# Nineteen pairs of projections by Strassen's seven products, ahead of an attention that takes more of the convolution's taps

## The chip, the cores and the metric

The kernel runs on one core of a Trainium2 chip. The core has a matrix engine (TensorE, PE in the profile; PEld is its weight load), three engines for elementwise work (VectorE is DVE, ScalarE is ACT, GpSimd is POOL), a queue engine that issues transfers (SyncE, SP), an on-chip memory of 128 partitions (SBUF) and an accumulator memory that TensorE writes (PSUM). The metric is the device time of one execution in microseconds; lower is better.

## The reference

One layer of a streaming encoder in float32 for 1024 prompt frames and 32 frames of running streams (TT = 1056 columns in all), model width 1024. What matters here:

```python
h = rmsnorm(x, norm_g)
cols = lambda a, w: h @ w_in[:, a:a + w]
q = rmsnorm(cols(OFF_Q, ATTN_WIDTH).reshape(B, T, N_HEADS, HEAD_DIM), q_g) * (HEAD_DIM ** -0.5)
k = rmsnorm(cols(OFF_K, ATTN_WIDTH).reshape(B, T, N_HEADS, HEAD_DIM), k_g)
v = cols(OFF_V, ATTN_WIDTH).reshape(B, T, N_HEADS, HEAD_DIM)
ga = cols(OFF_GA, ATTN_WIDTH)
u = cols(OFF_UA, CONV_WIDTH) * jax.nn.sigmoid(cols(OFF_UB, CONV_WIDTH))
...
ya = (o_attn.reshape(B, T, ATTN_WIDTH) * jax.nn.silu(ga)) @ w_pa
yb = (jax.nn.silu(layernorm(conv, ln_g, ln_b)) * jax.nn.silu(gb)) @ w_pb
m = jax.nn.sigmoid(ma) * ya + jax.nn.sigmoid(mb) * yb
return x + m @ w_out
```

`o_attn` is causal softmax attention of 16 heads of 64 with a bias from cumulated forget gates, `conv` a causal depthwise convolution of 31 taps over u.

## The kernel before

The activations lie transposed: channels on the partitions, the 1056 frames as columns. x is split once into a rounded part xh and the rest xl, eight groups of 128 channels each. Each of the nine input projections (q, k, v, ga, ub, ua, gb, ma, mb) has 1024 outputs, eight groups f of 128. One projection (g, f) is `steps`: three chunks of 352 columns, for each chunk eight groups kt of input channels, for each kt the three products wh·xh, wl·xh and wh·xl (`mms`, L102), 72 matmuls that accumulate in one PSUM bank a chunk. Its weights, 128 x 1024, arrive by one transfer of 512 KB (`load_raw`); ScalarE rounds them to wh (L91), POOL makes wl = raw - wh in three pieces of 384, 384 and 256 columns (L94).

The stages follow each other: x is prepared while u0 and u1 (ub and ua of group 0 and 1) run; then the value projection (L582, moving operand 260 columns) with u2 inside; k and q with u3 to u6 between; u7; eight groups of ga; the attention of 128 blocks (16 heads by 8 blocks of 128 frames) and four sample groups; then pa, pb and out, three projections of the same kind.

`beat()` stands behind every three matmuls. It counts a tick, runs what `later(n, fn)` set down for that tick, and pays out taps: each beat adds `pace["rate"]` to a credit, and while that is not negative the next tap or chore is issued. A tap is one of the 31 steps y = u[i:] * w + y of a convolution group, one VectorE instruction over 1086 columns (L258; the first of a group on ScalarE, L255), 30 a group, 240 in all. `sums(f)` adds a finished group to the layer norm's mean on VectorE (L235) and its squares on POOL (L241).

A q or k chunk is squared (ScalarE), split (L690 on VectorE), summed over heads by two matmuls with a matrix of ones (L697, L698), made into a reciprocal root (ScalarE), multiplied on (L704, VectorE, from PSUM) and split again, the low part on POOL (L715).

The order on TensorE, VectorE and ScalarE is the program's own up to the attention; from there it is fixed for TensorE alone, and a scheduler sets the rest. In the attention a block's scores (L905, L906) start three blocks ahead into one of two buffers psS; VectorE adds the mask (L908) and takes the maximum (L910), ScalarE the exponential (L913), VectorE the reciprocal (L915), POOL scales P (L916); TensorE turns P (L926) and multiplies it with V (L940). Between blocks `fill(4)` runs four beats of a filler: 22 further projections (gb, ma, six of mb) in all. The last two groups of mb follow the attention.

Of the kernel before, what the change touches and what calls it, by code (L numbers as in the profile page):

```python
# [30 lines left out]
NFILL = 22  # L31
R_U, R_V, R_QK, R_G, R_A = 0.25, 0.17, 0.19, 0.27, 0.12
# [16 lines left out]
def build(tc, xT, xt, wv, wf, ckT, cv, clT, stT, vec, cst, yT, kT, vO, lfO, cpT, csT):  # L49
# [19 lines left out]
    s_m = dram.tile([128, TT], F32, name="s_m")  # L69

    cp = pool("cp")
    wp = pool("wp", 2)
# [3 lines left out]
    rawp = [wp]  # L76
# [11 lines left out]
    def split_w(raw, offset=2000):  # L88
        with tc.high_priority(offset=offset):
            wh = wp.tile([128, KT, 128], F32R, name="wh", tag="wh")  # L90
            nc.scalar.copy(wh, raw)  # L91
            wl = wp.tile([128, KT, 128], F32R, name="wl", tag="wl")
            for k0, k1 in WSP:
                nc.gpsimd.tensor_sub(wl[:, k0:k1, :], raw[:, k0:k1, :], f32(wh[:, k0:k1, :]))  # L94
        return wh, wl
# [40 lines left out]
    def fetch():  # L136

        if plan:
            key = plan.pop(0)
            if not plan:  # L140
                rawp[:] = [wp]
# [28 lines left out]
    sg = pool("sg")  # L170

    def t352(name, bufs):
        return sg.tile([128, CH], F32, name=name, tag=name, bufs=bufs)

    pq = pool("pq", 1, space=PS)
    pps = ExitStack()
    pjA = pool("pjA", 4, stack=pps, space=PS)
# [15 lines left out]
    cvp = pool("cvp", 2, stack=pcv)  # L193
    us = {}
    taps = []
    cvt = [cvp]
# [9 lines left out]
    def shift_of(y):  # L206

        shift = cvp.tile([128, TT], F32, name="shift", bufs=1)
        ones = cvp.tile([128, 128], F32, name="ones", bufs=1)
# [8 lines left out]
        nc.sync.dma_start(s_m, shift)  # L218
# [28 lines left out]

    def conv_taps(f):
        u = us.pop(f)

        def tap(i):
            w = vec_t[:, V_WDW + f * KC + i:V_WDW + f * KC + i + 1]
            if i == 0:
                y = sides["y", f] = cvt[0].tile([128, CW], F32, name="y", tag="y")
# [4 lines left out]
            if f == 7:  # L259
                tc.keep_in_program_order(t)  # L260
            if i == KC - 1:
                kept(f, y)

        items = [lambda i=i: tap(i) for i in range(KC)]
        if f == 7:
            taps.extend(pend + items)
# [11 lines left out]
    def u_tile(f):  # L278
        if f > 2:
            pump(len(taps) - 66)  # L280
        u = us[f] = cvt[0].tile([128, UW], F32, name="u", tag="u", bufs=3 if f < 7 else 1)
# [4 lines left out]
    def u_done(f):  # L286
        u = us[f]
# [71 lines left out]
    os_t = cp.tile([128, 8, TS], F32, name="os_t")  # L359
# [116 lines left out]
    plan.extend([("ub", 1), ("ua", 1), ("v", 0), ("v", 1), ("ub", 2), ("ua", 2), ("v", 2), ("v", 3), ("ub", 3), ("ua", 3)])  # L476
    for f in range(8):
        if f in (2, 4, 6):
            plan.extend([("ub", 3 + f // 2), ("ua", 3 + f // 2)])
        plan.extend([("k", f), ("q", f)])  # L480
    plan.extend([("ub", 7), ("ua", 7)] + [("ga", f) for f in range(8)] + [("gb", 0)])
# [23 lines left out]
    prw = ExitStack()  # L505
    rxs = [pool(f"rx{i}", 1, stack=prw) for i in range(2)]
    rawp.extend(rxs)
# [3 lines left out]
    p2 = ExitStack()  # L511
    u7p = pool("u7p", 1, stack=p2, side="right")
    pv = ExitStack()
    zp = pool("zp", 1, stack=pv, side="right")
    z = zp.tile([128, 9, H], F32, name="z")
# [45 lines left out]
    for c in range(4):  # L561
        if c == 2:
            pace["rate"] = R_U
            u_proj(2, pj)
            while ("y", 0) not in sides or len(taps) > 62:
# [28 lines left out]
    fp = pool("fp", 1, stack=pv, side="right")  # L594
# [3 lines left out]
    def small(name):  # L598
        return fp.tile([128, NZ], F32, name=name, tag=name)

    lf = fp.tile([128, 9, H], F32, name="lf")
    lfs = lf, lf.rearrange("p a b -> p (a b)")

    def log_sigmoid():
        lf, lff = lfs
        az, ee, s2, ac = small("az"), small("ee"), small("s2"), small("ac")
# [19 lines left out]
        chores.extend([(0.3, op) for op in ops] + [(0.0, forget_sums)])  # L626
# [620 lines left out]
```

## Time and profile before

| | us |
|---|---|
| median of 3 runs | 1405.24 (1404.52 to 1405.70) |
| profiled execution, its own time | 1405.11 |
| span of the profiled execution | 1403.3 |
| x, u0, u1 | 0 to 72 |
| value projection with u2 | 72 to 193 |
| q, k, u3 to u6 | 193 to 503 |
| u7, ga | 503 to 613 |
| attention with 22 fillers | 613 to 1106 |
| two gates, pa, pb, out | 1106 to 1403 |

The span is the time from the first to the last instruction; the profiled execution's own time lies 1.8 us above it. A row of a group reads: line, engine, operation, tile written <- tiles read, shape, count | busy us, mean ns of one | idle time of the engine ahead of them and who ended it. A row of windows gives a stretch, its length, and for each engine its busy time and count. Matmuls overlap, so the duration of one is longer than the distance from one to the next.

### The profile page before, as it was taken

Reading aid. Unit: us, or ns where it says so; the run is one execution under the profiler, and the core shown is the slowest. Engines: PE = TensorE matmul, PEld = TensorE weight load, DVE = VectorE, ACT = ScalarE, POOL = GpSimd, SP = SyncE. Lnnn points to the kernel's source line nnn. Section 1 sums busy time; section 2 is a strip of 40 time slices with the busy share of each in tenths; the row PEclk is TensorE's granted clock in tenths of the full one; section 3 lists DMA queues with packets and bytes.
Section 4 is the critical chain, followed back from the end, with each engine's and each line's share of the span. In section 5 each row is a group of like instructions: output and inputs, shape, how many; then the busy total and the mean of one; then the engine's idle time right before and its main releaser. Section 6 shows DMA issues by size and latency. Waiting matters only on the chain.

```text
span 1403.3 us, 23422 instructions
## 1 busy us (share of the span) xinstructions
PE 1390.1 (99%) x8999; PEld 1303.6 (93%) x8999; DVE 866.0 (62%) x1199; ACT 604.2 (43%) x1180; POOL 617.5 (44%) x541
## 2 busy tenths in 40 slices
PE   8999999999999999999999999999999999999999
PEld 7999999999999999998888888878888999999998
DVE  6687787888898998646655656644444497132111
ACT  6322334646464642245454546544554455232100
POOL 2324254557585875343433433232332366254320
PEclk9999999999999999999999999999999999999999
DMA  4242333424342484335545546353532778444431
GB/s 181 92 141 92 119 108 99 160 76 142 106 152 92 138 194 150 111 100 129 148 107 160 146 136 177 101 154 109 155 115 73 276 254 271 143 138 142 150 108 47
DMA packets 102288, 192.77 MB, mean 137 GB/s; under 512 B 17248, under 2 KB 70368, under 8 KB 102176
## 3 DMA queue, kind: packets, MB, share of 16 engines
q1 hardware_dynamic: 102032, 191.21, 44.4%
q8 instruction: 71, 1.16, 0.4%
q14 instruction: 41, 0.34, 0.1%
q10 hardware_dynamic: 144, 0.07, 0.0%
HBM read 125.58 MB, written 65.64 MB: 136 GB/s over the span
## 4 chain that ended last, share of the span: by engine, by line
PE 92%; issue 3%; DVE 2%; ACT 2%; POOL 1%; DMA 1%; SPq 0%; ACTq 0%; POOLq 0%; DVEq 0%
PE pj L102 67%; PE pjv L582 7%; PE po L940 5%; PE ptr L926 4%; PE psS L905 3%; PE psS L906 2%; POOL wl L94 1%; PE pst L698 1%; PE pst L697 1%; PE po L885 0%; DVE y L1082 0%; PE ptx L427 0%; DMA xtok<-xt 0%; ACT xh L429 0%; PE pjs L541 0%
## 5 line engine op out<-in xcount | busy, mean ns | idle before, releaser
L102 PE MATMUL pj<-xh,wh 128*128 128x352 f32 (+2 forms) x1536 | 510.0, 332 | 1.7 <-ACT t L753 1.1
L102 PE MATMUL pj<-xh,wl 128*128 128x352 f32 (+2 forms) x1536 | 494.0, 322 | 1.9 <-POOL wl L94 1.9
L102 PE MATMUL pj<-xl,wh 128*128 128x352 f32 (+2 forms) x1536 | 495.5, 323 | 0.2
L94 POOL TENSOR_TENSOR wl<-raw,wh 128x384 fp32r<-128x384 f32 (+1 forms) x258 | 323.1, 1280 | 258.1 <-ACT wh L91 226.9
L258 DVE SCALAR_TENSOR_TENSOR y<-u,vec_t,y 128x1086 f32<-128x1086 f32 x240 | 382.5, 1594 | 23.7 <-ACT y L255 19.6
L102 PEld LDWEIGHTS pj<-xh,wh 128*128 128x128 f32 x1536 | 289.0, 188 | 10.2 <-ACT t L753 6.6
L102 PEld LDWEIGHTS pj<-xh,wl 128*128 128x128 f32 x1536 | 289.9, 189 | 2.5 <-POOL wl L94 2.2
L102 PEld LDWEIGHTS pj<-xl,wh 128*128 128x128 f32 x1536 | 289.1, 188 | 1.4 <-DVE xl L430 1.2
L916 POOL TENSOR_SCALAR P<-P,nm 128x128 f32<-128x128 f32 (+7 forms) x128 | 107.6, 842 | 283.3 <-DVE nm L915 216.9
L91 ACT CAST wh<-raw 128x1024 fp32r<-128x1024 f32 x86 | 90.1, 1048 | 111.2 <-PE pj L102 80.5
L913 ACT ACTIVATE P<-psS,nm 128x128 f32<-128x128 f32 (+7 forms) x128 | 95.4, 745 | 70.7 <-DVE nm L910 61.5
L910 DVE TENSOR_REDUCE nm<-psS 128x1 f32<-128x128 f32 (+7 forms) x128 | 96.8, 756 | 8.6
L908 DVE TENSOR_TENSOR psS<-psS,cmask 128x128 f32<-128x128 f32 x128 | 38.1, 297 | 100.3 <-PE psS L906 99.3
L929 ACT COPY pt<-ptr 128x512 f32<-128x512 f32 (+3 forms) x128 | 65.0, 508 | 75.8 <-PE ptr L926 75.1
L715 POOL TENSOR_TENSOR ql<-qn,qh 128x352 fp32r<-128x352 f32 (+1 forms) x48 | 66.0, 1374 | 68.0 <-ACT qh L714 54.9
L926 PE MATMUL ptr<-ident,P 128*128 128x128 f32 x576 | 84.2, 273 | 0.0
L940 PE MATMUL po<-pt,V 128*64 128x512 f32 (+1 forms) x384 | 75.8, 530 | 0.0
L926 PEld LDWEIGHTS ptr<-ident,P 128*128 128x128 f32 x576 | 69.1, 140 | 5.6 <-issue 0.4
L582 PE MATMUL pjv<-vwh,xh 128*128 128x260 f32 x256 | 72.5, 283 | 0.0
L582 PE MATMUL pjv<-vwl,xh 128*128 128x260 f32 x256 | 72.4, 283 | 0.0
L582 PE MATMUL pjv<-vwh,xl 128*128 128x260 f32 x256 | 72.3, 282 | 0.0
L905 PE MATMUL psS<-KB,QB 128*128 128x256 f32 (+2 forms) x192 | 70.1, 366 | 0.6 <-ACT t L751 0.6
(200 smaller groups left out, 2237.4 us busy)
## 6 DMA issues: line engine op xcount, KB each, us to landing
raw<-wf SPq DMA_DIRECT2D x88, 512.0 KB
QB<-s_q SPq DMA_DIRECT2D x32, 256.0 KB
KB<-s_k SPq DMA_DIRECT2D x32, 256.0 KB
kT<-qn SPq DMA_DIRECT2D x8, 528.0 KB
s_ga<-t SPq DMA_DIRECT2D x24, 176.0 KB
s_gb<-t SPq DMA_DIRECT2D x24, 176.0 KB
s_ma<-t SPq DMA_DIRECT2D x24, 176.0 KB
s_mb<-t SPq DMA_DIRECT2D x24, 176.0 KB
```

The source lines that it names most:

```text
L91: nc.scalar.copy(wh, raw)
L94: nc.gpsimd.tensor_sub(wl[:, k0:k1, :], raw[:, k0:k1, :], f32(wh[:, k0:k1, :]))
L102: nc.tensor.matmul(ps, a[:, kt, :], b(kt, sl), start=(first and n == 0), stop=(last and n == N - 1))
L258: t = nc.vector.scalar_tensor_tensor(y, u[:, i:i + CW], w, y, op0=ALU.mult, op1=ALU.add)
L582: nc.tensor.matmul(ps[:, :VC], a, b, start=(n == 0), stop=(n == 23))
L715: nc.gpsimd.tensor_sub(ql[:, :n], qn[:, o], f32(qh[:, :n]))
L905: nc.tensor.matmul(ps[:, b, :wm], QB[:, qsl], KB[:, ksl], start=True, stop=False)
L910: nc.vector.tensor_reduce(nm[:, 0:1], ps[:, :nb, :w], axis=AX.XY, op=ALU.max, negate=True)
L913: nc.scalar.activation(P[:, :nk].rearrange("p (b w) -> p b w", b=nb), ps[:, :nb, :w], AF.Exp, bias=nm[:, 0:1], accum_out=nm[:, 1:2])
L916: nc.gpsimd.tensor_scalar(P[:, :nk], P[:, :nk], nm[:, 2:3], 1.0, op0=ALU.mult, op1=ALU.mult)
L926: nc.tensor.transpose(pt[:, 128 * j:128 * j + 128], P[:, 128 * (4 * u + j):128 * (4 * u + j) + 128], ident)
L940: nc.tensor.matmul(po[64 * o:64 * o + 64, q0:], V[:, j + o, hd], p[:, j + o, q0:], start=(j == 0), stop=(j == njb - 2), skip_group_check=True)
```

## The change

Nineteen pairs of projections (ub and ua of groups 4 to 7; k and q of all eight; ga in four pairs; gb 0 to 5 in three), 38 of the 72 input projections, are computed in one stage ahead of the attention by seven products in place of eight (`products`). The weights of the two outputs of a pair and the two halves of the input channels make a 2 x 2 matrix of blocks a11, a12, a21, a22 (128 outputs by 512 channels); the two halves of channels and of columns (HT = 528) of x make b11 to b22. Each product is 2 column halves of HB = 264 by 4 kt by the same 3 terms, 24 matmuls, 168 a pair (L1013), 56 beats. Four PSUM tiles A to D of two banks hold the products; ScalarE takes out p1 and c11, VectorE n2, v3, c22, c21 and c12 (L988 to L1000, 528 columns each).

- *The operands t1 to t4* of x are built during u2 and u3, which now stand behind the whole value projection (`t_build`: joins xh + xl on POOL, sums and splits on VectorE and ScalarE). t1 is written over a quarter of xh and xl, which is kept in DRAM (s_x) and read back at the end of the stage (`restore`).
- *The weights.* Two raw tiles of a pair arrive as before. s2 and s1 start as a plain transfer of 256 KB each; three of the four sums s1, s2, s3 and s4 are then completed by DMAs that add while they write (`w_more`, L758, issued from POOL, 256 KB each, four a pair): s2 += a21, s3 += a11 (in the place of a21), s1 += a22, s2 += a22. The fourth, s4 = s2 + a12, is added by VectorE (`w_sum`, L763). `w_split` rounds each of the seven operands (512 columns) on ScalarE (L769) and takes the rest on POOL (L771), 22 beats ahead of its product.
- *k and q* are normed by halves of 528 columns from SBUF rather than by chunks of 352 from PSUM.
- *Taps.* 63 of the 240 are issued ahead of the pairs, 96 in them (rate 0.1 a beat), 81 in the attention (rate 0.3); before, 28 were issued in the attention. The u of groups 4 to 7 goes to DRAM and is read back when its taps come (`u_load`).
- *The attention* has 16 fillers in place of 22 (gb 6 and 7, ma, six of mb), `fill(3)` in place of `fill(4)`, and a fill ends with a chunk. Two gates follow it as before.

On POOL's order, at one k and q pair and what stands round it. Before (wl is the low half of a weight, ql that of q or k):

```order
L715 TENSOR_TENSOR ql<-qn,qh 128x352
L94 TENSOR_TENSOR wl<-raw,wh 128x384 x2
L94 TENSOR_TENSOR wl<-raw,wh 128x256
L715 TENSOR_TENSOR ql<-qn,qh 128x352
L721 TENSOR_SCALAR qs_t<-qn 128x32
L715 TENSOR_TENSOR ql<-qn,qh 128x320
```

Now (swl is the low half of a block, s_3613 and s_3635 are the tiles of s2 and s1, rawb that of s3, sa the low half of q or k):

```order
L758 DMA s_3613<-wf 128x512
L771 TENSOR_TENSOR swl<-rawb,swh 128x512 x2
L758 DMA s_3613<-wf 128x512
L771 TENSOR_TENSOR swl<-rawa,swh 128x512
L758 DMA rawb<-wf 128x512
L960 TENSOR_TENSOR sa<-qn,sb 128x528
L771 TENSOR_TENSOR swl<-s_3613,swh 128x512
L771 TENSOR_TENSOR swl<-rawb,swh 128x512
L960 TENSOR_TENSOR sa<-qn,sb 128x528
L771 TENSOR_TENSOR swl<-s_3635,swh 128x512
```

DMAs that wait for one another now stand between the subtractions.

On VectorE's order, among the k and q projections before (L258 is a tap):

```order
L704 SCALAR_TENSOR_TENSOR qn<-pj,vec_t,ri 128x352
L690 TENSOR_TENSOR sql<-sqf,sqh 128x352
L258 SCALAR_TENSOR_TENSOR y<-u,vec_t,y 128x1086
L704 SCALAR_TENSOR_TENSOR qn<-pj,vec_t,ri 128x352
L258 SCALAR_TENSOR_TENSOR y<-u,vec_t,y 128x1086
L690 TENSOR_TENSOR sql<-sqf,sqh 128x352
```

and in a pair of k and q now (L261 is a tap; psB to psD are the products' tiles):

```order
L988 TENSOR_TENSOR n<-psB,v 128x528
L261 SCALAR_TENSOR_TENSOR y<-u,vec_t,y 128x1086
L991 TENSOR_TENSOR v<-psC,n 128x528
L956 SCALAR_TENSOR_TENSOR qn<-qn,vec_t,sf 128x528
L994 TENSOR_TENSOR qn<-v,psD 128x528
L261 SCALAR_TENSOR_TENSOR y<-u,vec_t,y 128x1086
L937 TENSOR_TENSOR sa<-sf,sb 128x528
L261 SCALAR_TENSOR_TENSOR y<-u,vec_t,y 128x1086
L997 TENSOR_TENSOR qn<-psC,n 128x528
```

The evacuations, which free the tiles for the next products, stand among the taps, and the norm's two steps now read SBUF alone.

On VectorE's order in the attention, now (L1214 is the mask, L1216 the maximum, L1221 the reciprocal, L1235 a copy of turned P):

```order
L261 SCALAR_TENSOR_TENSOR y<-u,vec_t,y 128x1086
L1221 RECIPROCAL nm<-nm 128x1
L1214 TENSOR_TENSOR psS<-psS,cmask 128x128
L261 SCALAR_TENSOR_TENSOR y<-u,vec_t,y 128x1086
L1216 TENSOR_REDUCE nm<-psS 128x1
L1235 COPY pt_7728<-ptr_9106 128x128
L1214 TENSOR_TENSOR psS<-psS,cmask 128x128
L261 SCALAR_TENSOR_TENSOR y<-u,vec_t,y 128x1086
L1235 COPY pt_7728<-ptr_9135 128x2x128
L1216 TENSOR_REDUCE nm<-psS 128x1
```

A tap stands between a block's mask and its maximum, where before most blocks had none.

The diff, cut to its core:

```diff
@@ -28,8 +28,11 @@
...
-NFILL = 22
-R_U, R_V, R_QK, R_G, R_A = 0.25, 0.17, 0.19, 0.27, 0.12
+NFILL = 16
+R_U, R_V, R_T, R_S, R_A = 0.3, 0.25, 0.19, 0.1, 0.3
+HB = 264
+HT = 2 * HB
+SPILL = 4
...
@@ -623,137 +620,402 @@
...
+    def t_build(j):
+        b11, b12, b22 = [tm.tile([128, HT], F32, name=a, tag=a) for a in ("b11", "b12", "b22")]
+        t1 = t1f[:, j, :]
...
+        def lows():
+            joined(b11, 4 + j, LO)
+            nc.vector.tensor_sub(t3[1][:, j, :], b12, f32(t3[0][:, j, :]))
+
+        return [lambda: nc.vector.tensor_add(b11, f32(xh[:, j, LO]), f32(xl[:, j, LO])),
+                lambda: nc.vector.tensor_sub(t1, b11, b12),
+                lambda: (nc.vector.tensor_sub(b12, b12, b22), nc.scalar.copy(t3[0][:, j, :], b12)),
+                lambda: (nc.vector.tensor_add(b22, b22, t1), nc.scalar.copy(t2[0][:, j, :], b22)),
+                lows,
+                lambda: nc.vector.tensor_sub(t2[1][:, j, :], b22, f32(t2[0][:, j, :])),
+                lambda: (nc.vector.tensor_sub(b11, b11, b22), parts(t4, j, b11))]
...
+    others = [("ub", 4, "ua", 4), ("ub", 5, "ua", 5), ("ub", 6, "ua", 6), ("ub", 7, "ua", 7), ("ga", 0, "ga", 1),
+              ("ga", 2, "ga", 3), ("ga", 4, "ga", 5), ("ga", 6, "ga", 7)]
+    pairs = [("gb", 0, "gb", 1)]
+    for i in range(8):
+        pairs += [("k", i, "q", i), others[i]]
+    pairs += [("gb", 2, "gb", 3), ("gb", 4, "gb", 5)]
...
+    BP = 56
+    LEAD = 22
...
+    def raws_of(i):
...
+        g, f, g2, f2 = pairs[i]
+        with tc.high_priority(offset=2500):
+            w = W[i] = {}
+            for a, key in (("a", (g, f)), ("b", (g2, f2))):
+                w[a] = pw.tile([128, KT, 128], F32, name="raw" + a, tag="raw" + a, bufs=2)
+                nc.sync.dma_start(w[a], wf[WIDX[key]])
+            w["a11"], w["a12"] = w["a"][:, 0:4, :], w["a"][:, 4:8, :]
...
+    def w_first(i, dst, x):
+        w = W[i]
...
+        nc.sync.dma_start(w[dst], half(i, x))
...
+    def w_more(i, dst, x):
+        nc.gpsimd.dma_start(W[i][dst], half(i, x), accum_op=ALU.add)
...
+    def w_sum(i, dst, x, y, home):
+        w = W[i]
+        w[dst] = w[home]
+        nc.vector.tensor_add(w[dst], w[x], w[y])
...
+    def w_split(i, k):
+        raw = W[i][PROD[k][0]]
+        with tc.high_priority(offset=2000):
+            wh = pw.tile([128, 4, 128], F32R, name="swh", tag="swh", bufs=4)
+            nc.scalar.copy(wh, raw)
+            wl = pw.tile([128, 4, 128], F32R, name="swl", tag="swl", bufs=4)
+            nc.gpsimd.tensor_sub(wl, raw, f32(wh))
...
+    def prepare(i):
+        if i >= NP:
+            return
+        s = S0[0] + i * BP
+        for t, dst, x in ((50, "s2", "a11"), (46, "s1", "a21")):
+            at(s - t, lambda dst=dst, x=x: w_first(i, dst, x))
+        for t, dst, x in ((37, "s2", "a21"), (33, "s3", "a11"), (29, "s1", "a22"), (25, "s2", "a22")):
+            at(s - t, lambda dst=dst, x=x: w_more(i, dst, x))
+        at(s + 3, lambda: w_sum(i, "s4", "s2", "a12", "a21"))
+        for k in range(7):
+            at(s + 8 * k - (LEAD - 3 * (k == 1)), lambda k=k: w_split(i, k))
+
+    PROD = (("a11", "b11", 0, True, True), ("s2", "t2", 1, True, True), ("s3", "t3", 2, True, True),
+            ("s1", "t1", 3, True, True), ("a12", "b21", 0, False, True), ("a22", "t4", 2, False, True),
+            ("s4", "b22", 3, False, True))
...
+    def products(i):
+        s = S0[0] + i * BP
+        assert pace["tick"] == s
+        prepare(i + 1)
+        at(s + 34, lambda: raws_of(i + 2))
+        p = KIND.get(pairs[i][0], Gates)(s, *pairs[i])
...
+        def p1_out():
+            kept["v"] = ev.tile([128, HT], F32, name="v", tag="v")
+            nc.scalar.copy(two(kept["v"]), ps[0])
...
+        def n2_out():
+            kept["n"] = ev.tile([128, HT], F32, name="n", tag="n")
+            nc.vector.tensor_sub(two(kept["n"]), ps[1], two(kept["v"]))
...
+        def v3_out():
+            nc.vector.tensor_add(two(kept["v"]), ps[2], two(kept["n"]))
...
+        def c22(t):
+            nc.vector.tensor_sub(two(t), two(kept["v"]), ps[3])
...
+        def c21(t):
+            nc.vector.tensor_add(two(t), ps[2], two(kept["n"]))
...
+        def c12(t):
+            nc.vector.tensor_sub(two(t), ps[3], two(kept["n"]))
...
+        for t, fn in ((9, p1_out), (18, n2_out), (26, v3_out), (34, lambda: p.block(1, 1, c22)),
+                      (42, lambda: p.c11(ps[0])), (50, lambda: p.block(1, 0, c21)), (58, lambda: p.block(0, 1, c12))):
+            at(s + t, fn)
...
+        for k, (wn, xn, b, first, last) in enumerate(PROD):
+            wh, wl = W[i].pop(k)
+            oh, ol = OPS[xn]
+            if first:
+                ps[b] = bank("ABCD"[b])[:, :, :HB]
+            for c in range(2):
+                for kt in range(4):
+                    for n, (a, x) in enumerate(((wh, oh), (wl, oh), (wh, ol))):
+                        nc.tensor.matmul(ps[b][:, c, :], a[:, kt, :], x(kt, c), start=(first and kt == 0 and n == 0),
+                                         stop=(kt == 3 and n == 2), skip_group_check=not first)
+                    beat()
...
+    def restore():
+        for n, a in enumerate((xh, xl)):
+            nc.sync.dma_start(f32(a[:, 0:4, HI]), s_x[n])
...
+    at(e - 62, to_heads)
+    at(e - 19, restore)
...
     def fill(n):
...
-            next(flow, None)
+            if next(flow, None):
+                break
...
-            fill(4 if b.i > 2 or b.head.h != 8 else 0)
+            fill(3)
```

More of the change, by code (lines that the diff above doesn't have):

```diff
@@ L562, in build @@
         if c == 2:
-            pace["rate"] = R_U
-            u_proj(2, pj)
-            while ("y", 0) not in sides or len(taps) > 62:
+            while ("done", 0) not in sides:
                 pump(1)
@@ L815, in filler @@
+    fills = [("gb", f) for f in range(6, 8)] + [(g, f) for g in ("ma", "mb") for f in range(8)]
     def filler():
```

487 lines of the change are left out of this document (315 added, 172 removed).

## The prediction

> **What bounds the kernel now.** I read the page from the top: busy shares first, then the chain of waits, then the costliest groups, and after these the windows of the stages that the change touches.
>
> ```profile
> PE 1390.1 (99%) x8999; PEld 1303.6 (93%) x8999; DVE 866.0 (62%) x1199; ACT 604.2 (43%) x1180; POOL 617.5 (44%) x541
> PE 92%; issue 3%; DVE 2%; ACT 2%; POOL 1%; DMA 1%; SPq 0%; ACTq 0%; POOLq 0%; DVEq 0%
> PE pj L102 67%; PE pjv L582 7%; PE po L940 5%; PE ptr L926 4%; PE psS L905 3%; PE psS L906 2%; POOL wl L94 1%; PE pst L698 1%; PE pst L697 1%; PE po L885 0%; DVE y L1082 0%; PE ptx L427 0%; DMA xtok<-xt 0%; ACT xh L429 0%; PE pjs L541 0%
> L102 PE MATMUL pj<-xh,wl 128*128 128x352 f32 (+2 forms) x1536 | 494.0, 322 | 1.9 <-POOL wl L94 1.9
> ```
>
> TensorE is the bound: it is busy for 99% and carries 92% of the chain, 67% of it in the projections' one line, L102. The 322 ns of a matmul is no price, since neighbours overlap. The price is the pitch, which a stretch without any idle time gives as length over count. The next windows are of the matmuls of L102 (first) and of the value projection L582 (second), and then of all engines: PE, PEld, DVE, ACT and POOL busy, clock, DMA share.
>
> ```profile
> 1216.00:1306.00 90.00, 90.00 (x566) 90.00 (x565) 1.00 0.43 144
> 162.00:190.00 28.00, 28.00 (x235) 28.00 (x235) 1.00 0.39 130
> 400.00:500.00 100.00, 100.00 (x628) 99.97 (x627) 90.50 (x84) 57.55 (x108) 73.27 (x49) 1.00 0.38 127
> 613.00:1106.00 493.00, 491.77 (x3209) 417.89 (x3209) 265.88 (x586) 243.93 (x536) 170.89 (x194) 1.00 0.47 131
> ```
>
> So 352 columns cost 90.00/566 = 0.159 us and 260 columns 28.00/235 = 0.119 us: 0.43 ns a column between them. PE stands still for 0 of 100 us among the k and q projections and for 1.2 of 493 us in attention. Any matmul that goes is time that goes, as long as the others keep pace; the third row shows that VectorE, at 90.5%, is already close to not doing so.
>
> **What is removed.** A pair of ordinary projections is 144 matmuls of 352 columns, 144 x 0.159 = 22.9 us. A pair by seven products is 7 x 2 x 4 x 3 = 168 of 264 columns. Their pitch is 0.119 + 4 x 0.00043 = 0.121 us, so 20.3 us. The gain is 2.6 us a pair, 49 us for 19 pairs. The norm roots move the same columns as before (32 products of 264 for 96 of 352 become 128 of 264). The profiled execution took 1405.1 us (span 1403.3, some 1.8 us around it; the runs' median is 1405.2), so the floor is 1405.1 - 49 = 1356 us. Everything else is about what the other engines give back of these 49 us in the 19 x 20.3 = 386 us of the pairs, and next to them.
>
> **Weights: POOL.** Before, a projection's low half is three subtractions.
>
> ```profile
> L94 POOL TENSOR_TENSOR wl<-raw,wh x258: 717/1017/2383, 34.9 to 1379.8; 128x384 fp32r<-128x384 f32 x86, 128x256 fp32r<-128x256 f32 x43
> L532 POOL TENSOR_TENSOR vwl<-vraw,vwh x16: 1295/2136/2368, 62.0 to 158.5; 128x520 fp32r<-128x520 f32 x16
> 1331.51 2.68 POOL L94 TENSOR_TENSOR wl<-raw,wh 128x384 fp32r<-128x384 f32 x3 [9.41 <-ACT wh L91]
> 510.21 5.47 POOL L94 TENSOR_TENSOR wl<-raw,wh 128x384 fp32r<-128x384 f32 x3 [0.32 <-ACT wh L91]
> 523.15 5.12 POOL L94 TENSOR_TENSOR wl<-raw,wh 128x384 fp32r<-128x384 f32 x3 [7.47 <-ACT wh L91]
> 511.45 16.21 DVE L258 SCALAR_TENSOR_TENSOR y<-u,vec_t,y 128x1086 f32<-128x1086 f32 x10
> L258 DVE SCALAR_TENSOR_TENSOR y<-u,vec_t,y x240: 1326/1351/3541, 52.9 to 820.8; 128x1086 f32<-128x1086 f32 x120
> ```
>
> The smallest value of each row is the undisturbed one (min, median, max in ns): 717 ns for 256 columns and 1295 for 520, so 2.19 ns a column, 1.28 us for the new 512 columns. A pair's seven come to 9.0 us where two projections took 2 x 2.68 = 5.4.
>
> The same rows show how POOL and VectorE hinder each other: three subtractions take 2.68 us alone and 5.1 to 5.5 us while taps run. In the 16.21 us of ten taps POOL worked for 4.2 and 4.5 us. In the other 7.5 us, 5.5 taps fit at 1.35. So 8.7 us held 4.5 taps and about 4.9 subtractions, whose durations alone add to 6.1 + 4.4 = 10.5 us. They take turns and overlap by a sixth: two-input work of the two engines on SBUF adds up at some 0.85 of its time alone. The Trainium skill says the same in "SBUF — State Buffer", section "Who interferes with whom", and goes further: one of the two blocks fully until the other's instruction ends. By that the factor would be 1 and the stage's sum below 427 us, not 363; the trace agrees that they take turns, but has the factor at 0.85.
>
> The sum for 386 us, from rows here and below: POOL 133 x 1.28 = 170 for the weights, 32 x 1.3 = 41 for the low halves of k and q, 10 for the sums of squares, together 221; VectorE 96 taps (by its order of instructions) x 1.35 = 130, 64 steps of the norms x 0.73 = 47, 19 fourth sums x 0.71 = 13, products and means 16, together 206. That is 427 us, times 0.85 = 363, 94% of the stage. It fits, with next to nothing over.
>
> **The accumulating DMAs.** No instruction of the profile before issues a DMA from POOL, so X, what one of the four a pair keeps POOL, is unknown. The nearest rows are a DMA that SP issues, POOL's smallest instruction, and the rate at which DMAs moved data:
>
> ```profile
> 588.88 0.32 SPq L754 DMA_DIRECT2D s_ga<-t  x1
> 460.13 0.49 POOL L721 TENSOR_SCALAR ks_t<-qn 128x32 f32<-128x32 f32 x1
> DMA packets 102288, 192.77 MB, mean 137 GB/s; under 512 B 17248, under 2 KB 70368, under 8 KB 102176
> ```
>
> From below X is 0.32 us. From above it is the whole transfer of 256 KB, waited out at that mean rate: 0.262 MB / 137 GB/s = 1.9 us. I take 0.32 + 0.49 = 0.8 us. Taking turns as above, POOL waits about half of VectorE's 206 x 0.85 us, so its stage is 221 + 85 + 72 X: 364 us at X = 0.8, full at X = 1.1, 395 at 1.25 and 443 at 1.9. A bounded view from below, with no wait for VectorE, would leave it at 279. POOL works in order: a subtraction waits behind any DMA that itself waits for an earlier one onto the same tile, and PE waits for that subtraction 22 beats (8 us) after its due time. The reserve covers one late instruction, not a running deficit. At 94% on two engines I count half a microsecond of stall a pair, +9 us, with 0 and +40 as ends (POOL at 364 or at 424).
>
> The Trainium skill, "DMA: Bandwidth & Descriptors", section "Latency and other measured facts", gives about 1 us to a first byte for DMAs of this kind, by the time that descriptors take. Its estimate for X would then be 1, the stage 378 of 386 us, and the slip some 6 us more. No run here shows it yet.
>
> **Evacuation and ScalarE.** Five outputs of a pair of 528 columns go through VectorE from PSUM. The nearest row has 572 ns for 352 columns, so 0.86 each, 4.3 us a pair, without the shared port; VectorE is then 206 + 82 + waits of some 85 of 386 us, 97%. The banks have 8 to 14 beats (3 to 5 us) of reserve. ScalarE, at 58% in the third window, casts 7 x 512 columns a pair instead of 2 x 1024 (1.05 us each), 3.7 us against 2.1, which is 8% of a pair more. Neither is priced beyond the 9 us.
>
> ```profile
> L704 DVE SCALAR_TENSOR_TENSOR qn<-pj,vec_t,ri x24: 566/572/585, 226.5 to 482.3; 128x352 f32<-128x352 f32 x24
> L690 DVE TENSOR_TENSOR sql<-sqf,sqh x48: 488/561/1970, 220.8 to 489.3; 128x352 fp32r<-128x352 f32 x48
> L91 ACT CAST wh<-raw 128x1024 fp32r<-128x1024 f32 x86 | 90.1, 1048 | 111.2 <-PE pj L102 80.5
> ```
>
> (488 ns for 352 columns is where 0.73 for 528 and 0.71 for 512 come from.)
>
> **Ahead of the pairs.** In the 46 us of u2 and u3, twelve joins of 528 columns on POOL (1.31 each, 16), some 28 two-input steps on VectorE (0.73, 20), four weights (11), the first pair's splits (9) and a few taps (5) share the port: 61 x 0.85 = 52 us. The pairs start when the last operand is there, so +5 us; 0 if the joins run ahead, +12 if they take turns without overlap.
>
> **Attention.** It loses six fillers of 72 matmuls, which the 49 us hold already, and gets 81 taps instead of 28.
>
> ```profile
> L258 DVE SCALAR_TENSOR_TENSOR y<-u,vec_t,y 128x1086 f32<-128x1086 f32 x28 | 39.2, 1400 | 0.0
> L908 DVE TENSOR_TENSOR psS<-psS,cmask 128x128 f32<-128x128 f32 x125 | 37.2, 297 | 81.1 <-PE psS L906 80.1
> L910 DVE TENSOR_REDUCE nm<-psS 128x1 f32<-128x1024 f32 x16 | 19.6, 1224 | 1.1
> L910 DVE TENSOR_REDUCE nm<-psS 128x1 f32<-128x128 f32 (+7 forms) x128 | 96.8, 756 | 8.6
> L913 ACT ACTIVATE P<-psS,nm 128x128 f32<-128x128 f32 (+7 forms) x128 | 95.4, 745 | 70.7 <-DVE nm L910 61.5
> ```
>
> The window shrinks from 493 to 493 - 6 x 11.45 = 424 us. VectorE's other work there is 265.9 - 39.2 = 227 us; with 81 x 1.40 to 1.62 it is 340 to 358, and as the last tap stands at 78% of VectorE's rows, the first 331 us hold 290 to 308 of work, 88 to 93%. Before, VectorE was idle for 0.65 us ahead of each mask (81.1/125) and waited for the scores; now a tap often stands there instead. Scores may run two blocks ahead: 2 x 493/132 = 7.5 us before and 6.4 after, against a chain of mask, maximum and exponential of 0.3 + 1.2 us and some 1.2 more in the longest block (0.745 scaled as the maxima, 1224 to their mean of 756) and one or two taps of 1.4. Mostly that fits. I take 0.08 us a block, +10 us; 0 and +50 (a tap's whole time in the 36 blocks where nothing is left over) are the ends. The restored operand, the change of banks and the first head's loads add +3 (0 to 8).
>
> The sum: 1405.1 - 49 + 9 + 5 + 10 + 3 = 1383 us.
>
> **The rivals.**
> (a) *Nothing is given back* (for: PE stood still for 0 of 100 us at 90.5% of VectorE; against: 94% and 97% on engines that wait for one another). All ends at their lower values: 1356 to 1362 us.
> (b) *POOL becomes the bound, and the change is slower.* If X is 1.9, POOL needs 443 us in the 386 of the pairs: +57 in place of +9, 1431 us. It decides from where the slip is 49 - 18 = 31 us, X = 1.5. For it: two of the four are queued on one tile, and the engine works in order. Against: SP shows an issue at 0.32 us.
> (c) *The clock gives it back.* One row shows what a stall draws after itself.
>
> ```profile
> 591.23 0.43 PE L102 MATMUL pj<-xh,wl 128*128 128x352 f32 x1 [1.94 <-POOL wl L94]
> 592.40:595.80 3.40, 3.40 (x14) 3.40 (x13) 0.00 (x0) 0.00 (x0) 3.40 (x8) 0.51 0.99 353
> ```
>
> After 1.94 us of standing still the granted clock was 0.51 for 3.4 us, 1.7 us more lost. One such stall a pair costs 19 x 3.6 = 69 us: 1356 + 69 + 18 = 1443 us, and 8 of them still give 1403. The Trainium skill, "TensorE: Matmul & The Clock Gate", section "HAM oscillation — how this bites in real kernels", sets the mark at gaps above some 3.4 us; by it, stalls of half a microsecond to 2 us draw nothing after themselves, and this rival falls. The trace differs: 1.94 us was enough.
> (d) *Attention becomes VectorE's.* Taps ahead of the maxima stop PE: +50 in place of +10, 1423 us; half of that, 1403, is no change. For it: 88 to 93%. Against: the two blocks of lead.
>
> **How the numbers follow.** My forecast of 1383 us has 0.62, with its own range 1366 to 1400; (a) 0.12, (b) 0.10, (c) 0.06, (d) 0.10. The range 1357 to 1412 holds (a), the forecast and the lighter half of (d), and leaves out some 0.2. A measurement of this kernel tells 0.2%, 3 us, from no change: faster is the forecast, (a) and a little of (d), 0.78; the same 0.04; slower 0.18.
>
> **What would show it.** Right: a pitch of 0.121 us in the pairs, PE's idle time among them at 5 to 15 us in short pieces, released by the low weight halves on POOL more than by evacuations; attention near 430 us with its idle time ahead of scores, released by ScalarE's exponential. Wrong: a pitch above 0.125; POOL over 97% with the stalls in every pair (b); a granted clock under 0.97 in the pairs (c); attention above 450 us (d); DMA rows on POOL's queue of over 1.2 us.

## The result: 1486.9 us in place of 1404.9

The changed kernel takes 1486.86 us (median of 4 runs, 1479.95 to 1489.58), the kernel before on the same chip 1404.88. The ratio is 1.058 (95% interval 1.054 to 1.062): slower by 82 us, where 1383 was forecast and 1412 was the upper end of the range. The profiled execution's span is 1486.8 us.

The page of the kernel after, busy shares first, then two rows of the costliest groups (L771 is the low half of a weight block, L758 an accumulating DMA, whose own time is now a row of POOL):

```profile
PE 1384.1 (93%) x9487; PEld 1286.5 (87%) x9487; DVE 1021.5 (69%) x1311; ACT 647.1 (44%) x1209; POOL 760.6 (51%) x633
L771 POOL TENSOR_TENSOR swl<-rawb,swh 128x512 fp32r<-128x512 f32 x57 | 94.7, 1750 | 3.8 <-ACT swh L769 3.8
L758 POOL DMA_DIRECT2D s<-wf x57 | 53.7, 949 | 80.5 <-DMA s<-wf 57.3
L758 POOL DMA_DIRECT2D rawb<-wf x19 | 17.8, 946 | 25.9 <-DMA rawb<-wf 21.5 <-PE psD L1013 3.2 <-POOL sa L960 0.6
```

TensorE is busy 6 us less than before and idle 103 us instead of 13. Where it is idle, the windows of the stages show: the pairs, the attention, and what follows, all engines, clock, DMA share.

```profile
222.00:717.00 495.00, 437.95 (x3332) 430.44 (x3333) 390.40 (x322) 236.31 (x377) 331.20 (x271) 0.94 0.66 172
716.00:1163.00 447.00, 418.33 (x2689) 341.74 (x2689) 338.62 (x649) 229.46 (x513) 207.94 (x179) 0.97 0.49 139
1163.00:1487.00 324.00, 316.29 (x1945) 312.98 (x1941) 109.36 (x139) 97.97 (x126) 127.57 (x110) 0.99 0.51 168
```

The pairs' matmuls start 0.122 us apart (the median distance of their starts in the trace). That is 168 x 0.122 = 20.5 us a pair against 22.9, and 19 x 2.4 = 46 us are gained. But 3332 matmuls of 0.122 us are 406 us, and the pairs take 495: 57 us of standing still, and most of the rest under a mean granted clock of 0.94. The same window of the kernel before, from the first score to the last value, and what follows it:

```profile
605.00:1095.00 490.00, 488.42 (x3185) 414.20 (x3185) 268.13 (x589) 245.12 (x539) 173.98 (x196) 1.00 0.46 128
1095.00:1403.00 308.00, 303.36 (x1872) 301.65 (x1872) 115.35 (x139) 94.84 (x122) 126.03 (x107) 1.00 0.52 173
```

Six fillers less (69 us) should have left 421 us of attention. It took 447, although 63 matmuls of fillers (10 us) slipped behind it: 36 us lost, 29 of them standing still. What follows is 16 us longer, 10 for those matmuls. The balance is -46 + 88 + 36 + 6 = +84 us, against 83.5 between the spans. It leaves out two terms that cancel. The pairs begin at 222 us, 6 us later than the same work of the kernel before, which took 193 us and 22.9 for u3. And the 412 us of q, k, u3 to u7 and ga before (193 to 605) were some 7 us longer than their matmuls need, 34 x 11.45 + 96 x 0.159 = 405 us.

Who ended TensorE's waits, after (us in all, times, the longest in us):

```profile
PE psB L944 <- DVE sa L937: 24.2, 10, 3.3
PE psS L1211 <- ACT P L1219: 23.1, 10, 6.3
PE psB L943 <- DVE n L988: 9.0, 5, 4.1
PE psC L1013 <- POOL swl L771: 8.9, 3, 4.0
PE psA L1013 <- DVE u L314: 5.4, 1, 5.4
```

In the pairs it is less the weights than the norm's sums over heads (L943, L944), which stand in PE's queue ahead of the next product and wait for VectorE. One such stall, by the timeline of the pair from 461 us on (between the dots, rows are left out):

```profile
478.52 0.69 DVE L994 TENSOR_TENSOR qn<-v,psD 128x528 f32<-128x528 f32 x1
...
480.37 0.88 POOL L758 DMA_DIRECT2D s<-wf  x1 [3.62 <-DMA s<-wf]
480.58 2.54 DVE L937 TENSOR_TENSOR sa<-sf,sb 128x528 fp32r<-128x528 f32 x1 [1.38 <-ACT sb L934]
480.83 0.28 PE L943 MATMUL psB<-sb,bones 128*128 128x264 f32 x1
480.98 1.57 POOL L771 TENSOR_TENSOR swl<-rawa,swh 128x512 fp32r<-128x512 f32 x1
...
483.18 0.59 PE L944 MATMUL psB<-sa,bones 128*128 128x264 f32 x1 [2.07 <-DVE sa L937]
483.57 0.42 PE L943 MATMUL psB<-sb,bones 128*128 128x264 f32 x1
...
484.01 0.42 PE L1013 MATMUL psD<-xh,swh 128*128 128x264 f32 x1
```

POOL stood for 3.62 us at the second addition onto s2, until the first had landed, then issued it and went on with a subtraction. VectorE's split of the squares, some 0.7 us alone, met that subtraction, with which it takes turns, and took 2.54. PE waited 2.07 us for it, and its matmuls are 0.42 us long after that, 0.28 before: half the clock.

Most of these stalls have a second link. In seven of the ten at L944, 19 of the 24 us, VectorE's split had itself been standing still. The tile sa, into which it writes, has two buffers. POOL writes the low half of a normed k or q into the same tile (L960), and a transfer stores that to DRAM. VectorE's row, and the longest case on POOL, VectorE and PE:

```profile
L937 DVE TENSOR_TENSOR sa<-sf,sb 128x528 fp32r<-128x528 f32 x32 | 43.8, 1370 | 52.5 <-DMA s_q<-sa 45.6 <-ACT sb L934 6.9
550.80 1.84 POOL L960 TENSOR_TENSOR sa<-qn,sb 128x496 fp32r<-128x496 f32 x1
557.13 0.71 DVE L937 TENSOR_TENSOR sa<-sf,sb 128x528 fp32r<-128x528 f32 x1 [10.48 <-DMA s_q<-sa]
557.90 0.39 PE L944 MATMUL psB<-sa,bones 128*128 128x264 f32 x1 [3.03 <-DVE sa L937]
```

POOL was done at 552.64 us, the store of sa released VectorE 4.5 us later. It had stood for 10.48 us by then, with an evacuation and a tap behind it in its queue. So what is late on POOL also reaches PE through this tile. No run gave sa a third buffer.

### The profile page after: what moved, and what is told of

It is laid out like the page before. It is cut to its first block, busy times and chain, and to the rows that moved or that the text cites. A ratio compares the mean times of both kernels' runs of the same rounds, so it can differ in the third digit from the quotient of the medians.

```text
span 1486.8 us, 24992 instructions
## 1 busy us (share of the span) xinstructions
PE 1384.1 (93%) x9487; PEld 1286.5 (87%) x9487; DVE 1021.5 (69%) x1311; ACT 647.1 (44%) x1209; POOL 760.6 (51%) x633
## 5 line engine op out<-in xcount | busy, mean ns | idle before, releaser
L261 DVE SCALAR_TENSOR_TENSOR y<-u,vec_t,y 128x1086 f32<-128x1086 f32 x240 | 400.4, 1669 | 4.7 <-ACT y L258 2.6
L99 POOL TENSOR_TENSOR wl<-raw,wh 128x384 fp32r<-128x384 f32 x141 | 159.8, 1161 | 197.5 <-ACT wh L96 163.7
L107 PE MATMUL pj<-xh,wh 128*128 128x352 f32 (+3 forms) x624 | 217.8, 349 | 3.9 <-ACT t L1113 1.6
L107 PE MATMUL pj<-xl,wh 128*128 128x352 f32 (+3 forms) x624 | 204.7, 328 | 0.2 <-DVE xl L439 0.2
L107 PE MATMUL pj<-xh,wl 128*128 128x352 f32 (+3 forms) x624 | 204.0, 327 | 0.6 <-POOL wl L99 0.6
L107 PEld LDWEIGHTS pj<-xh,wh 128*128 128x128 f32 x624 | 119.3, 191 | 9.6 <-ACT t L1113 3.4
L107 PEld LDWEIGHTS pj<-xl,wh 128*128 128x128 f32 x624 | 119.5, 192 | 1.8 <-DVE xl L439 1.8
L107 PEld LDWEIGHTS pj<-xh,wl 128*128 128x128 f32 x624 | 119.9, 192 | 1.3 <-POOL wl L99 0.9
L1216 DVE TENSOR_REDUCE nm<-psS 128x1 f32<-128x128 f32 (+7 forms) x128 | 96.3, 752 | 5.5
L1013 PE MATMUL psA<-xh,swh 128*128 128x264 f32 x304 | 90.6, 298 | 7.7 <-DVE u L314 5.4
L771 POOL TENSOR_TENSOR swl<-rawb,swh 128x512 fp32r<-128x512 f32 x57 | 94.7, 1750 | 3.8 <-ACT swh L769 3.8
L758 POOL DMA_DIRECT2D s<-wf x57 | 53.7, 949 | 80.5 <-DMA s<-wf 57.3
L1235 ACT COPY pt<-ptr 128x512 f32<-128x512 f32 (+3 forms) x128 | 64.7, 505 | 64.3 <-PE ptr L1232 63.3
L1013 PE MATMUL psA<-xh,swl 128*128 128x264 f32 x304 | 90.0, 296 | 0.5 <-POOL swl L771 0.5
L1013 PE MATMUL psA<-xl,swh 128*128 128x264 f32 x304 | 89.6, 295 | 0.0
L1013 PE MATMUL psD<-xh,swh 128*128 128x264 f32 x304 | 88.6, 291 | 0.1
L1013 PE MATMUL psD<-xl,swh 128*128 128x264 f32 x304 | 88.0, 289 | 0.0
```

The costliest lines, as they stand in the source:

```text
L107: nc.tensor.matmul(ps, a[:, kt, :], b(kt, sl), start=(first and n == 0), stop=(last and n == N - 1))
L261: t = nc.vector.scalar_tensor_tensor(y, u[:, i:i + CW], w, y, op0=ALU.mult, op1=ALU.add)
L758: nc.gpsimd.dma_start(W[i][dst], half(i, x), accum_op=ALU.add)
L771: nc.gpsimd.tensor_sub(wl, raw, f32(wh))
L1013: nc.tensor.matmul(ps[b][:, c, :], a[:, kt, :], x(kt, c), start=(first and kt == 0 and n == 0), stop=(kt == 3 and n == 2), skip_group_chec ...
L1216: nc.vector.tensor_reduce(nm[:, 0:1], ps[:, :nb, :w], axis=AX.XY, op=ALU.max, negate=True)
```

## The experiments

Two theories of the pairs. **Q**: POOL's queue. Each accumulating DMA keeps POOL and makes it wait. **V**: VectorE has too much to do with 96 taps among evacuations and norms, and the DMAs only stand where POOL would have waited anyhow. All runs are compared by the length of the pairs (first to last of their 3192 matmuls: 494 us after) and by their time; line numbers are those of each run's own kernel. Each length is that of one execution. Three runs below that leave the pairs as they are have 491 us, so differences of 4 us tell nothing.

**Without the accumulating DMAs.**

```diff
-        nc.gpsimd.dma_start(W[i][dst], half(i, x), accum_op=ALU.add)
+        pass
```

> Leaves out the 76 accumulating DMAs (s1, s2, s3 are then single blocks, so the pairs' outputs are not the projections). Theory Q (POOL's queue): each of these DMAs keeps POOL 0.95 us and makes it wait another 1.4 us for an earlier one to land, 179 us of the 495 us of the pairs; what comes late on PE (the norm's sums, the low weight halves) is late by that. By Q the pairs fall from 495 to 415 to 430 us, the time to some 1410 us, and the granted clock in the pairs rises to 0.98 or more. Theory V (VectorE): 96 taps among evacuations and norms are what is too much; the DMAs stand where POOL would have waited anyhow. By V the pairs stay at 470 us or more, the time at 1460 or more.

1429.16 us, the pairs 438 us, standing still for 20 us in them. The window of the pairs:

```profile
220.00:658.00 438.00, 417.76 (x3323) 415.09 (x3324) 373.31 (x322) 239.50 (x377) 311.03 (x200) 0.97 0.46 151
```

52 to 56 us came from the DMAs, more than half of the 88 lost. The pairs are 8 us above Q's range and 32 us below V's. 32 us of loss stay with the sums gone, so Q is not all of it.

**Without the taps in the pairs.** `tap` returns ahead of its VectorE instruction from the first pair to the last (the last tap of a group excepted).

> Leaves out the taps on VectorE that fall into the pairs (the convolution of three groups is then wrong); the DMAs stay as they are. V: PE's stalls in the pairs go almost wholly, 495 to 410 to 425 us, the time to some 1410. Q: POOL's waits for landings stay (over 80 us), the subtractions get shorter by the port alone (1.67 to 1.3 us each), and the pairs stop at 450 to 475 us, the time at 1440 to 1465.

1464.09 us, the pairs 470 us: V's number is missed by 45 us, Q's is met. The taps cost 21 to 24 us, though VectorE's busy time fell by 177 us:

```profile
222.00:692.00 470.00, 426.22 (x3323) 421.27 (x3324) 213.69 (x228) 239.36 (x377) 304.64 (x271) 0.95 0.70 180
```

VectorE at 45% still lets PE stand, 43 us in all. The largest part, 16.5 us, stands again behind VectorE's split of the squares, which waited 60.6 us in all for the store of sa that POOL's low half precedes.

**Without either.**

> Leaves out both the accumulating DMAs and the taps in the pairs. If the two costs come from two queues of their own, they add: 495 - 56 - 24 = 415 us. If both act through the one port of POOL and VectorE, the second gives more than alone once the first is gone, 405 to 412 us, close to the 406 us that 3330 matmuls of 0.122 us need. If a third cost is behind both, the pairs stay above 425 us.

The pairs take 411 us, 3 us of them standing still, and the granted clock is back at 0.99:

```profile
219.00:631.00 412.00, 407.43 (x3321) 406.33 (x3322) 193.39 (x228) 243.99 (x377) 249.49 (x201) 0.99 0.49 160
```

56 + 24 = 80 of 83 us, and with both gone the products run at their pitch. By the numbers set down, 411 us falls to the case of one port and misses the plain sum of 415 by 4 us; that is no more than the scatter between equal pairs, so the run doesn't tell whether the two costs only add. This run's time, 1402.76 us, equals the kernel before (ratio 0.9998, 0.9986 to 1.0010), with work left out. So even pairs almost without a loss would not have made this kernel faster: the attention and what follows it give back 39 of the 46 us (445.8 + 319.5 us against 489.6 + 305.0 - 68.7: from the first score to the last value, from there to the last matmul, less six fillers), the pairs' own remainder 5.

**The DMAs spread.** The beats become 51 and 50 for the plain loads, 42, 39, 36 and 23 for the additions.

> The same DMAs, spread: the second one onto s2 starts 19 beats behind the first in place of 12, and the first three 3 to 7 beats earlier. Only POOL's waiting for a landing shall go (106 us in all by the profile after), not the 0.95 us each. Q: waiting falls under 50 us, the pairs by 20 to 40 us, the time to 1450 to 1470 us. V: the pairs stay within 8 us of 495 and the time at 1480 to 1490.

1484.15 us, the pairs 490. But POOL's waiting did not fall either, 76 us at the DMAs onto s1 and s2 against 80: the plain loads into the same tiles then came too late. The edit did not take away what it was to take away, so it says nothing for V.

**One DMA less.** The second addition onto s2 is left out.

> Leaves out the fourth DMA of a pair, the second one onto s2 (the pairs' outputs are then not the projections): 19 issues and the wait for the first to land go. If waiting is the larger part, POOL's idle time ahead of L758 falls from 106 us to under 50 and the pairs by 25 to 40 us, much more than a quarter of the 56 us that all four cost; if each issue counts alike, the pairs fall by 10 to 16 us.

1475.1 us, the pairs 482: 9 to 13 us, about a quarter of the 56. POOL's waiting ahead of the rest is still 84 us, since it now stands at the next one:

```profile
L758 POOL DMA_DIRECT2D s<-wf x38 | 36.8, 973 | 44.4 <-DMA s<-wf 31.0 <-PE psC L1013 3.4 <-PE psB L1013 2.9
L758 POOL DMA_DIRECT2D rawb<-wf x19 | 17.3, 923 | 39.6 <-DMA rawb<-wf 39.1 <-POOL b L697 0.5
```

**Four more DMAs of 8 numbers a partition, that nobody waits for.**

```diff
+        nc.gpsimd.dma_start(tiny[t], wf[WIDX[g, f]][:, 0, 0:8], accum_op=ALU.add)
```

> Adds four more accumulating DMAs a pair, of 8 numbers a partition onto tiles of their own that nothing waits for, two beats behind each of the four: 76 times the cost of an issue and nothing else. If the issue itself (0.95 us of POOL) is what hurts, POOL has 72 us more to do and the pairs grow from 495 by 20 to 35 us (the 179 us taken away in the run without them gave 56, 0.31 us each). If the harm is in waiting for a landing, the pairs stay within 8 us.

1522.27 us, 35 more. They did not spread over the pairs: nothing held them back, and the scheduler put all 76 between 165 and 323 us, 41 of them ahead of the pairs.

```profile
L771 POOL DMA_DIRECT2D tiny<-wf x76: 856/1213/2559, 165.5 to 322.6; - x76
DMA to landing us min/median/max: 2.2/3.1/6.9
```

So it is no even dose, and the pairs as such grew by 13 us only, which is neither theory's number. But the start of the attention moved by 37 us for 76 issues of 1.27 us in the mean; 24 us of that lie ahead of the pairs, where POOL makes the operands. The issue alone, with a few bytes behind it and no wait, costs about half a microsecond each where POOL is loaded.

**The sums by VectorE, or by POOL,** from the raw tiles, with no DMA and no plain load:

```diff
-        for t, dst, x in ((37, "s2", "a21"), (33, "s3", "a11"), (29, "s1", "a22"), (25, "s2", "a22")):
-            at(s - t, lambda dst=dst, x=x: w_more(i, dst, x))
+        for t, dst, x, y in ((37, "s1", "a21", "a22"), (33, "s2", "s1", "a11"), (29, "s3", "a21", "a11")):
+            at(s - t, lambda dst=dst, x=x, y=y: w_add(i, dst, x, y))
```

> No accumulating DMA and no plain load of s1 and s2: VectorE adds s1 = a21 + a22, s2 = s1 + a11 and s3 = a21 + a11 from the raw tiles, 57 additions more. Q: POOL gets 179 us back, VectorE pays 57 x 1.6 = 91 us on the shared port; the pairs come to 440 to 465 us, the time to 1430 to 1455. V: VectorE gets 91 us more of what was too much already, the pairs go to 510 us or more, the time over 1500.

> The three sums by POOL additions from the raw tiles, no accumulating DMA. If POOL's time is what counts, 57 x 1.3 to 1.7 us = 75 to 97 us take the place of 179 us: the pairs come to 455 to 470 us against 465 with VectorE's additions and 494 with DMAs. If waiting for a landing was the whole harm, the pairs come close to the 438 us without any sum, 438 to 448 us.

VectorE: 1460.19 us, the pairs 465, the upper end of Q's range; the time is 5 us above Q's, and V is missed by 45 us. POOL: 1488.0 us, the pairs 491, no better than the DMAs. The windows of the pairs, with VectorE's additions,

```profile
222.00:686.00 464.00, 426.36 (x3319) 419.37 (x3320) 419.60 (x376) 238.18 (x377) 313.71 (x200) 0.96 0.36 121
```

and with POOL's:

```profile
222.00:710.00 488.00, 429.77 (x3284) 421.13 (x3285) 389.40 (x320) 235.30 (x376) 407.92 (x253) 0.94 0.34 113
```

The run with POOL's additions misses both theories' numbers. 57 additions, 2.0 us each beside VectorE's work, bring POOL's busy time from 311 us without any sum to 408, and that costs as much as 76 DMAs with 71 us of issuing and 106 of waiting. So it seems to matter that POOL is kept, not by what; and VectorE, at 90% busy, still had more room than POOL.

**Two DMAs that wait for none,** s2 = s1 + a11 on VectorE (with the late sums of below, whose pairs take 491 us).

> Two accumulating DMAs a pair, of which none waits for another (s1 += a22, s3 += a11), s2 = s1 + a11 by VectorE, and the late sums. If what hurts is each DMA with its share of POOL's queue, 13 us for each of the four, the pairs come to 470 to 480 us, between 494 and the 465 of VectorE's additions. If only the chain on s2 hurts (plain load, first, second, split), the two cost nearly nothing, and one addition costs VectorE a third of 27 us: 445 to 455 us, better than all additions.

1455.82 us, the pairs 475, as a like cost of each DMA says, and not as the chain on s2 says. POOL waited 84 us at these 38 DMAs, now for the raw weights and the plain loads. By 4, 3, 2 and 0 DMAs a pair: 491 to 494, 482, 475 (with one addition more on VectorE) and 438 us. How much of the 13 us is the issue and how much the waiting, no run could separate, since the waiting moved along to whichever load came next.

The link over sa shows in all these runs. PE's waits behind VectorE's split of the squares are 24.2, 22.3 and 22.8 us with four, three and two DMAs and 15.1 us with POOL's additions, but 1.6 us without any sum and 2.6 us with VectorE's. POOL's low half of the first q or k of a pair ends 7.9 us (the median) behind the product that it splits with four DMAs, 10.6 with POOL's additions and 5.8 in the other two. VectorE's next split into the same buffer began 4.5 us after that with four DMAs, and 2.8 to 3.0 us after it in the three runs without, so the stores land later among the DMAs, too. How much of the loss a third buffer would have saved, no run shows.

**Without the taps in the attention.**

> Leaves out the 81 taps on VectorE in the attention; the layer norm's sums stay there. If the taps ahead of the maxima stop PE, its idle time in the attention falls from 28.7 to under 8 us and the attention from 447 to 415 to 425 us, the time to 1450 to 1460. If the cause is the shorter filler between blocks (three beats in place of four) or the sums, which wait for a store, idle time stays at 18 us or more and the attention over 433 us.

1463.77 us, 4 us above the range for the taps; the attention 425 us, standing still for 14.6 us, between the two cases. The taps cost 22 us, and the sums are behind part of the rest. Most heads now run without a gap, with the same three beats of filler, so the shorter filler is not the cause. Two places are left, and this is one, VectorE's timeline ahead of a stall of 5.2 us:

```profile
788.13 0.54 DVE L1237 COPY pt<-ptr 128x384 f32<-128x384 f32 x1
791.83 2.37 DVE L227 TENSOR_TENSOR y<-y,shift 128x1024 f32<-128x1024 f32 x2 [3.17 <-DMA s_y<-y]
794.13 0.18 DVE L1163 TENSOR_TENSOR pf<-pf,smask 128x32 f32<-128x32 f32 x1
794.23 0.28 DVE L1216 TENSOR_TENSOR psS<-psS,cmask 128x128 f32<-128x128 f32 x1
```

The layer norm's first sum overwrites y and so waits 3.17 us for y's own store, with the masks behind it in the queue.

**The sums later.** They are put behind 16 taps of the next group in place of 4; the second version also keeps them in the program's order.

> As the changed kernel, but the layer norm's sums of the last groups stand 16 taps behind the group's start in place of 4, so that the store of y on which the first of them waits has landed. If VectorE's wait for that store makes the long stalls of the attention (6.3 us, 2.5 us), idle time there falls from 28.7 to 22 us or less and the time by 5 to 10 us. If the sums' own 4 us of work in one go make them, idle time stays within 3 us of 28.7.

> The run before did not move the sums: a scheduler sets VectorE's order in the attention, and the first sum stood behind the same tap. Here the first sum is kept in the program's order, behind the 15th tap of the next group. If the wait for the store of y makes the two long stalls (6.3 us ahead of one sum, 2.5 and 1.9 at the next), idle time in the attention falls from 28.7 to 22 us or less and the time by 5 to 10 us; if the work of the sums in one go does, idle time stays within 3 us of 28.7 and the stalls only move.

The first version changed nothing (1485.69 us, 28.0 us of standing still): the scheduler left the sums at the same tap, so it tested nothing. The second moved them: 1473.45 us, the attention 432 us in place of 447, and the wait for the store nearly gone. The groups of the first sum, after and then in this run, and this run's attention:

```profile
L227 DVE TENSOR_TENSOR y<-y,shift 128x1024 f32<-128x1024 f32 (+1 forms) x16 | 15.2, 984 | 5.7 <-DMA s_y<-y 5.7
```

```profile
L227 DVE TENSOR_TENSOR y<-y,shift 128x1024 f32<-128x1024 f32 (+1 forms) x16 | 14.9, 968 | 1.6 <-DMA s_y<-y 1.6
```

```profile
711.00:1144.00 433.00, 411.97 (x2698) 337.29 (x2698) 338.76 (x650) 229.11 (x513) 213.72 (x179) 1.00 0.51 144
```

Moving the sums took 4 us of VectorE's waiting away and 15 us of attention: the stalls of 6.3 and 2.5 us are 1.2 and none, and the granted clock is 1.00 in place of 0.97. The time fell by 13 us, where 5 to 10 were expected.

**Both remedies; and all of it left out.**

> VectorE's three additions in place of the accumulating DMAs, and the late sums in the attention. If the two causes are independent, 1460 less 12 to 13 us gives 1446 to 1449 us, with the pairs at 465 and the attention at 432. If the attention's gain came from VectorE's order as a whole, it is smaller here, 1452 us or more.

> Leaves out the accumulating DMAs and every VectorE tap from the first pair on (pairs and convolution are then not the reference's). If what has been found adds up, 1402.8 us of the run with neither in the pairs less the 20 to 22 us of the taps in the attention gives 1380 to 1384 us, with 14 us of idle time left at the layer norm's sums. If the products' own gain of 49 us were not there, the time would stay over 1395 us even so.

With VectorE's additions and late sums: 1446.41 us (pairs 464, attention 432), as the two alone add up; the best complete version here, 1.031 times the kernel before (1.027 to 1.034). Without DMAs and taps: 1385.11 us (ratio 0.988, 0.985 to 0.991), 1 us above the range, the pairs 412 us, the attention 426. The gain of the products is there: 1403.3 - 46, plus 6 lost in the pairs, plus 22 in and behind the attention, is 1385, and that run's span is 1384.7.

## Why the prediction was wrong, step by step

- *The gain of 49 us*: right to 3 us. The pitch is 0.122 us where 0.121 was worked out, so 46.
- *X, the price of an accumulating DMA, 0.8 us*: too small by its larger part. An issue's record lasts 0.95 us, near it; its place in the queue is shorter still, for in the 52 cases of 76 in which POOL's next instruction did not have to wait, that one started 0.61 us after it (the median). But POOL stands 106/76 = 1.4 us ahead of each, so 2.0 to 2.35 in all. That is more than the upper end of 1.9. The text named one reason (two additions on one tile, an engine that works in order) under rival (b) and took no price for it. Only 33 of the 106 us are of that kind. It did not see the others: 46 us stand ahead of the first additions onto s1 and s2, 22 of them by the trace until the plain load had landed, and 27 ahead of those onto s3, 21 of them until the raw weight had. Putting 2.0 to 2.35 into its own formula gives 306 + 72 X = 450 to 475 us for POOL, 19 to 44 below what the pairs took.
- *"At 94% on two engines I count half a microsecond of stall a pair"*: the step that failed. It was 57 us of standing still and some 27 of slow clock, 4.4 us a pair. The fill of 94% was worked out from durations and the mean factor of 0.85 alone. It has no term for a queue that stands and holds up the next one: POOL at a DMA, VectorE at the store of sa behind POOL, PE at the norms' sums behind VectorE. Half a microsecond was not worked out from a row. 33 of the 57 us stood at the norms' sums, waiting for VectorE; the low weight halves, which the text expected ahead of PE, ended 9 us in their longest row. Without DMAs, POOL was busy for 71% and VectorE for 85% of the pairs, and PE still lost 32 us.
- *Rival (b), POOL as the bound, 1431 us, 0.10*: the nearest of the rivals in its mechanism, and the price was too low. Its mark, "POOL over 97%", was wrong: POOL was busy for 67% and waiting for 21%. A queue that waits is as full as one that works.
- *Rival (c), the clock*: no rival, but a share in every case. 54 us of matmul time in the pairs ran at half the clock, which is 27 us lost, after stalls of 2 to 5 us; the granted clock of 0.94 is under the 0.97 that was to be the sign.
- *Attention, +10*: it lost 36 us and 6 behind it. Taps ahead of the maxima made 22, as (d) said, and the store in front of the sums made 15. This second wait was not seen at all. Before, the sums of all groups but the last ran ahead of the attention; after, three groups' sums stand in it. The prediction counted the 81 taps but not the sums that moved with them.
- *Ahead of the pairs, +5*: right in size, 6 us. The first product waited 5.4 us of it for an evacuation on VectorE, which stood in the queue behind the building of the operands.

## What to carry to other kernels

On a kernel whose TensorE is never idle, a saving of matmuls is worth what the other engines can still take: add up the time of each queue with its waits, not its busy time, and ask of each instruction that is put into an in-order queue what it waits for and who stands behind it. A DMA that adds into memory is not free for the engine that issues it: here each took 0.6 to 1 us of POOL and stopped it for 1.4 us more, mostly until the load ahead of it had landed, and the same sums on the engine with room cost half as much. A wait travels through every tile that two engines share, so count the buffers of such a tile against the time that its store takes. When work is moved into another stage, everything that is tied to it moves along (here the sums behind the taps, with a wait for a store), and each has to be costed where it lands.

## What the runs showed of the hardware that was not expected

An accumulating DMA of 256 KB onto s1 or s2 took 3.7 to 7.8 us from issue to landing (median 5.0), one of 4 KB still 2.2 to 6.9 (median 3.1).

```profile
L758 POOL DMA_DIRECT2D s<-wf x57: 847/884/1287, 210.5 to 683.9; - x57
DMA to landing us min/median/max: 3.7/5.0/7.8
```

The issue itself does not slow VectorE: the 10 taps of the pairs that ran beside an issue and no other POOL work took 1.34 us in the mean, as the 23 that ran beside nothing, while the 35 beside POOL's other work took 1.89. The clock halved at once after a stall of 2.07 us (0.42 us in place of 0.28 for the matmuls above), but not after every such stall: 4 us at a granted clock of 1.00 followed those of 2.49, 2.93 and 2.95 us that ended at 433, 607 and 659 us. The Trainium skill, "TensorE: Matmul & The Clock Gate", section "HAM oscillation — how this bites in real kernels", puts the mark at gaps above some 3.4 us; this case does not agree, as 2.07 us were enough, and here 57 us of stalls drew 27 us of slow clock after them, half as much again.
